# Hybrid encoder step on one core: sums of up-projection weight blocks made step by step through the mixers' phase instead of in the first up block

## The chip, the cores and the metric

The kernel runs on one core of a Trainium2 chip. The metric is device time in microseconds (us) of one execution, the median of several runs; lower is better. The core has five engines, each with its own in-order queue: PE (TensorE, matrix products), DVE (VectorE), ACT (ScalarE), POOL (GpSimd) and SP (SyncE), which here issues nearly all DMAs.

## The reference

One layer of an encoder, for a prompt of 2048 tokens and a sample group of 8 x 16 tokens, all in float32:

```python
h = rms_norm(x, norm_g[0])
z = h @ w_in                      # 1024 -> 3592, split into attention and mLSTM operands
att = band_attention(...)         # 8 heads x 64, own chunk and 8 chunks before
hb  = mlstm_sequence(...)         # 4 heads x 128, blockwise recurrence
x = x + rms_norm(concat(rms_norm(att), gated hb) @ w_out, norm_g[1])
u = rms_norm(x, norm_g[2]) @ w_up # 1024 -> 2 * 2816 (gate, up)
y = causal depthwise conv of width 3 over u, plus b_conv
x = x + rms_norm((gelu(gate of y) * (up of y)) @ w_down, norm_g[3])
```

What matters for the change is `w_up`. The kernel does its product with Strassen's method in Winograd's form: a 2 x 2 scheme of weight blocks a11, a12, a21, a22 is multiplied in 7 products instead of 8, and for this it needs four sums of weight blocks: s1 = a21 + a22, s2 = s1 - a11, s3 = a11 - a21, s4 = a12 - s2.

## The kernel before

**Phases.** The mixers' phase runs 28 groups: two halves of the tokens times 14 column groups of `w_in` (`seq`, the loop over `n_`). The matrix products of a group are the main stream. After each piece of it (`for u, (pe, dve) in enumerate(it)`, one pass per four inner products) the program calls `pump(pe, dve)` with the PE and DVE time that the piece is reckoned to cost. `pump` then takes steps from two pipelines, attention (`att_stream`) and mLSTM (`mem_stream`), as long as the reckoned DVE time stands below `SHARE` (0.615) times the reckoned PE time, two steps at most per call. Work that is put into `ahead` is made in the same pass and is counted in the same account: splitting the next group's weights, norms of the second half.

After the 28 groups comes the output projection (`project`, run through `out`): 17 tiles of 128 rows in the order 0 to 7, the sample tile (16), 8 to 15. For each tile `load` fetches the mixed row (`mr`, from `mixd`), `norm` scales it, `turn_rows` transposes it (`mT` on PE, then `mt` on ACT and DVE), 48 products make two halves (`wo`) which DVE copies out (`mx`), and the new row goes to `x2d`. The pipelines are pumped there too. When `load` comes to tile 8, `drain()` empties both pipelines at one go and `open_ffn()` closes the pools of the mixers' phase, opens those of the FFN phase, and starts `h2_units`, which fetches the rows `x2r` from `x2d` and transposes them (`h2T`) for the up product.

The FFN phase runs three blocks of tokens (b = 0, 1, 2), each with an up part (22 steps f: 7 products of 12 matmuls, then conv and GELU) and a down part.

**The weight blocks.** `load_quads(b, f, g)` fetches the 128 x 512 blocks ("quads") of step f for the first four products (g = 0) or the last three (g = 1). In block 0 it loads the four raw blocks, makes the four sums on DVE (L1274), stores each of them to `wsd[f]` in DRAM (L1276) and hands a12, a22 and s4 on through `raws`. In blocks 1 and 2 it loads all seven quads: three raw ones from `w_up` (L1269) and four sums from `wsd`. `load_up` then splits each quad into a high and a low part, on ACT (L1257) and DVE (L1258).

**Order.** The program is written in emission order. The Tile framework then places the instructions of each engine by its own reckoning of when they can run, so an instruction may stand earlier or later in its queue than it was written; `tc.keep_in_program_order` fixes a DMA's place. On the chip each engine works through its queue strictly in that order.

Of the kernel before, what the change touches and what calls it, by code (L numbers as in the profile page):

```python
# [17 lines left out]
P = 128  # L18
# [10 lines left out]
NF = 22  # L29
# [15 lines left out]
def hymba_step(ctx: ExitStack, tc: tile.TileContext, I: dict, O: dict):  # L45
# [1104 lines left out]
    def load_group(gi):  # L1150
# [19 lines left out]

        return h, l, steps()

    def norm_steps(half):

        for ci, tiles in enumerate(HALVES[half]):
            ch = phT.tile([P, 2, KT, 384], F32R, tag="hT", name=f"hT{half}_{ci}", bufs=3)
            chunks.append(ch)
            for j, t in enumerate(tiles):
                norm_tile(t, ch, j, ps_big)
                yield 0.9, 2.5  # L1180
# [9 lines left out]
        pass  # L1190
    next(norms)
    load_bias()
    for n_, (half, gi) in enumerate(seq):
        wh, wl, _ = pend
        split = iter([])
        if n_ + 1 < len(seq):
            pend = load_group(seq[n_ + 1][1])
            split = pend[2]
        g = GROUPS[gi]
        i = int(g[2])  # L1200
        nm = f"{g}_{half}"
        if g[:2] == "va":
            it = group_rows(wh, wl, half, chunks, vd[i], nm, 264 if gi == 0 else 256,
                            [O["v_prompt"][i], O["v_sample"][i].unsqueeze(1)])
        elif g[:2] == "qk":
            it = group_T(wh, wl, half, chunks, [qTd[i], kTd[i]], [-(DA ** -0.5), None], nm,
                         [None, [O["k_prompt"][i], O["k_sample"][i]]])
        elif g[:2] == "qb":
            it = group_T(wh, wl, half, chunks, [[t_[:, c, :] for t_ in qkbd[i]] for c in range(2)],
                         [None, DH ** -0.5], nm)  # L1210
        else:
            it = group_rows(wh, wl, half, chunks, vobd[i], nm)
        if half == 0 and gi == 13:
            chunks = []
            norms = norm_steps(1)
        if n_ == len(seq) - 1:
            out = project([0, 1, 2, 3, 4, 5, 6, 7, SAMPLE, 8, 9, 10, 11, 12, 13, 14, 15])
            split = w_out_steps()
            next(split)
            next(out)  # L1220
        for u, (pe, dve) in enumerate(it):
            ahead = []
            if n_ < len(seq) - 1 or u >= 6:
                ahead.append(next(split, (0.0, 0.0)))
            if n_ == len(seq) - 1 and u == 12:
                ahead.append(next(out))
            if (half == 0 and gi == 13 and u >= 6 and u % 2 == 0) or (gi == 0 and u % 2 == 0):
                ahead.append(next(norms, (0.0, 0.0)))
            pump(pe + sum(a[0] for a in ahead), dve + sum(a[1] for a in ahead))
        for _ in split:  # L1230
            pass
        if gi == 0:
            if half == 0:
                nc.sync.dma_start(bgate, I["b_gate"].broadcast_to([P, 8]))
                nc.sync.dma_start(gatt, I["g_att"])
                heads.append(build_bias)
                mems.append(lambda: prep(prep_sample()))
            mems.append(lambda half=half: prep(prep_prompt(half)))
        if g[:2] == "qk":
            attention(i, half)  # L1240
            if half == 0 and i == 3:
                heads.insert(len(heads) % 4, lambda: attention_sample(0, EARLY))
            if half == 1 and i == 0:
                heads.insert(len(heads) % 4, lambda: attention_sample(EARLY, DB))
        if g[:2] == "vo":
            mems.append(lambda i=i, half=half: mlstm(i, half))
            if half == 0:
                mems.append(lambda i=i: mlstm_sample(i))
# [8 lines left out]
        nc.scalar.copy(h, r)  # L1257
        nc.vector.tensor_tensor(l, r, h, op=ALU.subtract)  # L1258

    raws = {}  # L1260

    def load_quads(b, f, g):

        src = lambda i: I["w_up"][f][:, i * 512:(i + 1) * 512]
        if b == 0 and g == 0:
            q = []
            for i in range(4):
                q.append(quad(f"wu{f}_{i}"))
                nc.sync.dma_start(q[i], src(i))  # L1269
            a11, a12, a22, a21 = q  # L1270
            s1, s2, s3, s4 = [quad(f"ws{f}_{i}") for i in range(4)]
            for o, x, y, op in ((s1, a21, a22, ALU.add), (s2, s1, a11, ALU.subtract), (s3, a11, a21, ALU.subtract),
                                (s4, a12, s2, ALU.subtract)):
                nc.vector.tensor_tensor(o, x, y, op=op)  # L1274
            for i, o in enumerate((s2, s3, s1, s4)):
                nc.sync.dma_start(wsd[f][:, i * 512:(i + 1) * 512], o)  # L1276
            raws[f] = [a12, a22, s4]
            return [a11, s2, s3, s1]
        if b == 0:
            return raws.pop(f)  # L1280
        kept = lambda i: wsd[f][:, i * 512:(i + 1) * 512]
        out = []
        for i, s_ in enumerate([[src(0), kept(0), kept(1), kept(2)], [src(1), src(2), kept(3)]][g]):
            r = quad(f"wu{b}_{f}_{g}_{i}")
            nc.sync.dma_start(r, s_)
            out.append(r)
# [399 lines left out]
```

## Time and profile before

| what | value |
|---|---|
| three runs | 2813.98 us median, 2809.69 to 2816.1 |
| span of the profiled execution, first to last instruction | 2794.3 us |
| start, first group's norms | 0 to 56.0 |
| mixers' phase, groups 1 to 27 | 56.0 to 1044.4 |
| output projection | 1044.4 to 1317.6 |
| up part, block 0 | 1317.6 to 1645.9 |
| down part, block 0 | 1645.9 to 1840.1 |
| up part, block 1 | 1840.1 to 2158.1 |
| down part, block 1 | 2158.1 to 2356.0 |
| up part, block 2 (320 columns instead of 384) | 2356.0 to 2626.1 |
| down part, block 2 | 2626.1 to 2794.3 |

The page gives no time of its own for the profiled execution beside its span. The median of the runs lies 2813.98 - 2794.3 = 19.7 us above the span: start and end of the execution, which the instructions don't cover. The stages are cut at the first matmul of each kind. A time such as 1195.58 is counted from the span's start.

In a row of a view, `L1274 DVE TENSOR_TENSOR ws<-wu,wu 128x512 ... x44 | 30.2, 687 | 7.1 <-DMA ...` means: line 1274, on DVE, writes `ws` from `wu` and `wu`, 44 times, 30.2 us in sum, 687 ns each; before them the engine was idle 7.1 us, mostly for a DMA. PEld is the loading of weights into PE, which overlaps the products. PEclk is the clock that TensorE was granted, as a share of full speed.

### The profile page before, as it was taken

Reading aid. Unit: us, or ns where it says so; the run is one execution under the profiler, and the core shown is the slowest. Engines: PE = TensorE matmul, PEld = TensorE weight load, DVE = VectorE, ACT = ScalarE, POOL = GpSimd, SP = SyncE. Lnnn points to the kernel's source line nnn. Section 1 sums busy time; section 2 is a strip of 40 time slices with the busy share of each in tenths; the row PEclk is TensorE's granted clock in tenths of the full one; section 3 lists DMA queues with packets and bytes.
Section 4 is the critical chain, followed back from the end, with each engine's and each line's share of the span. In section 5 each row is a group of like instructions: output and inputs, shape, how many; then the busy total and the mean of one; then the engine's idle time right before and its main releaser. Section 6 shows DMA issues by size and latency. Waiting matters only on the chain.

```text
span 2794.3 us, 47075 instructions
## 1 busy us (share of the span) xinstructions
PE 2728.0 (98%) x16587; PEld 2551.0 (91%) x16587; DVE 1873.5 (67%) x3442; ACT 1408.9 (50%) x2836; POOL 449.9 (16%) x876
## 2 busy tenths in 40 slices
PE   8999999999999999999999999999999999999998
PEld 7999999998899998878999988899999778999887
DVE  5344455656456678666989986467777854888855
ACT  4445555644356676443454556345445543555543
POOL 1000010212000012344212210011111310222221
PEclk9999999999999999999999999999999999999999
DMA  5544355557554555255645455644444774555585
GB/s 189 157 123 126 111 173 157 171 159 212 165 159 147 159 183 165 91 194 210 192 164 173 162 171 173 220 148 157 151 153 154 259 262 158 169 180 177 182 309 195
DMA packets 313419, 486.04 MB, mean 174 GB/s; under 512 B 55427, under 2 KB 150623, under 8 KB 313055
## 3 DMA queue, kind: packets, MB, share of 16 engines
q1 hardware_dynamic: 274590, 449.21, 50.2%
q10 hardware_dynamic: 38592, 33.83, 3.6%
q8 instruction: 130, 2.13, 0.3%
q14 instruction: 107, 0.87, 0.1%
HBM read 359.36 MB, written 126.70 MB: 174 GB/s over the span
## 4 chain that ended last, share of the span: by engine, by line
PE 52%; DVE 4%; DMA 2%; issue 2%; ACT 1%; POOL 1%; SPq 0%; DVEq 0%; POOLq 0%; ACTq 0%
PE uec L95 6%; PE uec L96 6%; PE uec L97 5%; PE dn L97 4%; PE dn L96 3%; PE dn L95 3%; PE ua L97 3%; PE ua L95 3%; PE ua L96 3%; PE dnm L95 2%; PE dnm L97 2%; PE dnm L96 2%; PE wo L95 2%; PE wo L96 2%; PE wo L97 2%
## 5 line engine op out<-in xcount | busy, mean ns | idle before, releaser
L95 PE MATMUL uec<-B,wuh 128*128 128x384 f32 (+1 forms) x720 | 236.6, 329 | 5.6 <-DVE uu L1499 4.7
L96 PE MATMUL uec<-B,wuh 128*128 128x384 f32 (+1 forms) x720 | 235.4, 327 | 0.0
L97 PE MATMUL uec<-B,wul 128*128 128x384 f32 (+1 forms) x720 | 233.5, 327 | 0.0
L1258 DVE TENSOR_TENSOR gl<-gr,gh 128x768 fp32r<-128x768 f32 (+3 forms) x141 | 118.3, 846 | 158.6 <-ACT gh L1257 158.2
L1257 ACT CAST gh<-gr 128x768 fp32r<-128x768 f32 (+3 forms) x141 | 102.1, 736 | 211.5 <-PE dn L96 178.3
L1257 ACT CAST wuh<-wu 128x512 fp32r<-128x512 f32 x255 | 141.8, 617 | 91.2 <-PE uec L96 87.3
L95 PE MATMUL dn<-wdh,gh 128*128 128x512 f32 x466 | 182.6, 392 | 2.4 <-DVE ug L1410 2.4
L96 PE MATMUL dn<-wdl,gh 128*128 128x512 f32 x466 | 183.6, 394 | 0.0
L97 PE MATMUL dn<-wdh,gl 128*128 128x512 f32 x466 | 168.5, 396 | 0.0
L1258 DVE TENSOR_TENSOR wul<-wu,wuh 128x512 fp32r<-128x512 f32 x255 | 164.7, 685 | 2.8 <-DMA x2d<-mx 2.8
L393 DVE CUSTOM_DVE_ANT_0 tmp<-s,nb 128x640 f32<-128x640 f32 (+4 forms) x128 | 94.5, 738 | 95.8 <-PE s L383 95.2
L95 PE MATMUL vo<-wi_h,hT 128*128 128x256 f32 x544 | 156.0, 287 | 0.6 <-DVE mt L199 0.6
L97 PE MATMUL vo<-wi_h,hT 128*128 128x256 f32 x544 | 156.4, 287 | 0.0
L96 PE MATMUL vo<-wi_l,hT 128*128 128x256 f32 x544 | 155.5, 286 | 0.0
L95 PEld LDWEIGHTS uec<-B,wuh 128*128 128x128 f32 x720 | 135.3, 188 | 9.9 <-DVE uu L1499 6.7
L96 PEld LDWEIGHTS uec<-B,wuh 128*128 128x128 f32 x720 | 135.5, 188 | 0.1
L97 PEld LDWEIGHTS uec<-B,wul 128*128 128x128 f32 x720 | 135.2, 188 | 0.0
L95 PE MATMUL qk<-hT,wi_h 128*128 128x384 f32 (+1 forms) x384 | 128.5, 335 | 4.3 <-ACT qk_st L224 3.4
L406 DVE TENSOR_TENSOR ptl<-pt,pth 128x640 fp32r<-128x640 f32 (+4 forms) x128 | 93.7, 738 | 57.6 <-ACT pth L405 56.5
L394 ACT ACTIVATE tmp<-tmp,mn 128x640 f32<-128x640 f32 (+4 forms) x128 | 97.6, 763 | 63.0 <-DVE mn L393 60.5
L96 PE MATMUL qb<-hT,wi_h 128*128 128x384 f32 (+1 forms) x384 | 128.0, 333 | 0.0
L96 PE MATMUL qk<-hT,wi_h 128*128 128x384 f32 (+1 forms) x384 | 127.6, 332 | 0.0
(409 smaller groups left out, 8901.6 us busy)
## 6 DMA issues: line engine op xcount, KB each, us to landing
wu<-in_w_up SPq DMA_DIRECT2D x220, 256.0 KB, 3.9
wu<-wsd SPq DMA_DIRECT2D x176, 256.0 KB, 4.0
wdr<-in_w_down SPq DMA_DIRECT2D x132, 256.0 KB, 5.5
gr<-gd SPq DMA_DIRECT2D x78, 384.0 KB, 3.5
wi_raw<-in_w_in SPq DMA_DIRECT2D x52, 512.0 KB, 4.0
wsd<-ws SPq DMA_DIRECT2D x88, 256.0 KB, 2.8
gd<-g SPq DMA_DIRECT2D x44, 384.0 KB, 3.4
kraw<-kTd SPq DMA_DIRECT2D x112, 128.0 KB, 3.3
```

The lines of the kernel that those rows point to most:

```text
L95: nc.tensor.matmul(out, ah, bh, start=start, stop=False, skip_group_check=onto)
L96: nc.tensor.matmul(out, ah, bl, start=False, stop=False, skip_group_check=onto)
L97: nc.tensor.matmul(out, al, bh, start=False, stop=stop, skip_group_check=onto)
L393: nc.vector.tensor_tensor_reduce(o_, s_, b_, 1.0, 3e38, ALU.add, ALU.min, accum_out=mn)
L394: nc.scalar.activation(tmp[:, :n], tmp[:, :n], AF.Exp, bias=mn, scale=-1.0, accum_out=rsum[:, i % 4, hh:hh + 1])
L406: nc.vector.tensor_tensor(s.ptl[:, sl, qc], ptv, s.pth[:, sl, qc], op=ALU.subtract)
L1257: nc.scalar.copy(h, r)
L1258: nc.vector.tensor_tensor(l, r, h, op=ALU.subtract)
```

## The change

A new generator `weight_sums` makes the sums of all 22 steps during the mixers' phase. For each f it loads the four raw blocks by one DMA of 1 MB into one buffer (`wsum`, 8 KB per partition, one of it), waits five passes, makes the four sums in place on DVE, each in a pass of its own (the last shares its pass with the store), stores the whole buffer to `wsd[f]` by one DMA of 1 MB, and waits six passes: 15 passes per f, 330 in all. One step of it is taken in each pass of the groups from the second one on, and its DVE time (0.69 reckoned per sum) goes into `pump`'s account. What is left at the end of the last group is made there.

In block 0, `load_quads` no longer loads raw blocks for sums, makes sums or stores them: it loads the seven quads as the other blocks do. The order of the sums within `wsd[f]` is another, and `load_quads` follows it. Beside that the program is built with `dynamic_dma_scratch_size=1024`, which leaves more of each partition to the kernel.

```diff
+    def weight_sums():
+        for f in range(NF):
+            t = pr.tile([P, 4, 512], F32, tag="wsum", name=f"wsum{f}", bufs=1)
+            tc.keep_in_program_order(nc.sync.dma_start(t, I["w_up"][f].rearrange("p (a n) -> p a n", a=4)))
+            for _ in range(5):
+                yield 0.0, 0.0
+            a11, a12, a22, a21 = [t[:, i, :] for i in range(4)]
+            for o, x, y, op in ((a22, a21, a22, ALU.add), (a21, a11, a21, ALU.subtract), (a11, a22, a11, ALU.subtract),
+                                (a12, a12, a11, ALU.subtract)):
+                nc.vector.tensor_tensor(o, x, y, op=op)
+                if o is not a12:
+                    yield 0.0, 0.69
+            nc.sync.dma_start(wsd[f].rearrange("p (a n) -> p a n", a=4), t)
+            yield 0.0, 0.69
+            for _ in range(6):
+                yield 0.0, 0.0
...
+    sums = weight_sums()
     for n_, (half, gi) in enumerate(seq):
...
+            if n_:
+                ahead.append(next(sums, (0.0, 0.0)))
...
+        if n_ == len(seq) - 1:
+            for _ in sums:
+                pass
...
-    raws = {}
-
     def load_quads(b, f, g):
         src = lambda i: I["w_up"][f][:, i * 512:(i + 1) * 512]
-        if b == 0 and g == 0:
-            q = []
-            for i in range(4):
-                q.append(quad(f"wu{f}_{i}"))
-                nc.sync.dma_start(q[i], src(i))
-            a11, a12, a22, a21 = q
-            s1, s2, s3, s4 = [quad(f"ws{f}_{i}") for i in range(4)]
-            for o, x, y, op in ((s1, a21, a22, ALU.add), (s2, s1, a11, ALU.subtract), (s3, a11, a21, ALU.subtract),
-                                (s4, a12, s2, ALU.subtract)):
-                nc.vector.tensor_tensor(o, x, y, op=op)
-            for i, o in enumerate((s2, s3, s1, s4)):
-                nc.sync.dma_start(wsd[f][:, i * 512:(i + 1) * 512], o)
-            raws[f] = [a12, a22, s4]
-            return [a11, s2, s3, s1]
-        if b == 0:
-            return raws.pop(f)
         kept = lambda i: wsd[f][:, i * 512:(i + 1) * 512]
         out = []
-        for i, s_ in enumerate([[src(0), kept(0), kept(1), kept(2)], [src(1), src(2), kept(3)]][g]):
+        for i, s_ in enumerate([[src(0), kept(0), kept(3), kept(2)], [src(1), src(2), kept(1)]][g]):
...
-    nc = bacc.Bacc("TRN2", target_bir_lowering=False, num_devices=1)
+    nc = bacc.Bacc("TRN2", target_bir_lowering=False, num_devices=1, dynamic_dma_scratch_size=1024)
```

How the change moves instructions is seen at two places. The first is the DVE queue where the last attention unit ends and the FFN phase is opened, in the middle of the output projection. `attst3` is the last attention result; `x2r0`, `x2r3` are the first rows of the FFN phase; `mr8`, `mr9` are tiles 8 and 9 being scaled for the projection; a copy of `wo7` or `wo16` into `mx` follows 24 projection products of that tile on PE. Before:

```order
L436 TENSOR_TENSOR attst3_3_15157<-ao3_3_15152,rinv3_3_15150 128x512
L1014 COPY mx7_15107<-wo7_1_15191 128x512
L1042 MEMSET halo_15181 128x88
L1014 COPY mx16_15253<-wo16_0_15255 128x512
L1079 SCALAR_TENSOR_TENSOR x2r0_15187<-x2r0_15187,n2_0_rs_15212,g2_15183 128x1024
L1079 SCALAR_TENSOR_TENSOR x2r3_15189<-x2r3_15189,n2_3_rs_15219,g2_15183 128x1024
L1026 SCALAR_TENSOR_TENSOR mx7_15107<-mx7_15107,n1_7_rs_15240,norm_row1_13133 128x1024
L1014 COPY mx16_15253<-wo16_1_15332 128x512
L985 TENSOR_SCALAR mr8_15185<-mr8_15185,att8_rs_15250 128x512
```

And now, the same place of the DVE queue:

```order
L436 TENSOR_TENSOR attst3_3_15326<-ao3_3_15321,rinv3_3_15319 128x512
L1042 MEMSET halo_15335 128x88
L1079 SCALAR_TENSOR_TENSOR x2r0_15341<-x2r0_15341,n2_0_rs_15366,g2_15337 128x1024
L1079 SCALAR_TENSOR_TENSOR x2r3_15343<-x2r3_15343,n2_3_rs_15373,g2_15337 128x1024
L1026 SCALAR_TENSOR_TENSOR mx7_14958<-mx7_14958,n1_7_rs_15394,norm_row1_12943 128x1024
L985 TENSOR_SCALAR mr8_15339<-mr8_15339,att8_rs_15404 128x512
L1026 SCALAR_TENSOR_TENSOR mx16_15407<-mx16_15407,n1_16_rs_15516,norm_row1_12943 128x1024
L1100 TENSOR_TENSOR B0_0_15358<-b110_15427,B0_0_15358 128x4x128
L985 TENSOR_SCALAR mr9_15468<-mr9_15468,att9_rs_15526 128x512
```

The three copies out of `wo7_1`, `wo16_0` and `wo16_1` have moved ahead of the last attention units, and the scaling of tile 9 has come up behind that of tile 8. On PE the last attention transpose (`ao3`) was followed by the rest of `wo7_1` and all of `wo16` before; those three rows and the first of `wo16` were

```order
L67 MATMUL ao3_3_15152<-ident_69,attT3_3_14865 128x128 x2
L95 MATMUL wo7_1_15191<-wo6_13608,mt7_14889 128x512
L96 MATMUL wo7_1_15191<-wo6_13608,mt7_14889 128x512
L97 MATMUL wo7_1_15191<-wo6_13608,mt7_14889 128x512
L95 MATMUL wo16_0_15255<-wo0_13395,mt16_15099 128x512
```

and now it is followed at once by what hangs on the FFN phase's first rows and on tiles 8 and 9:

```order
L67 MATMUL ao3_3_15321<-ident_69,attT3_3_15177 128x128 x2
L1087 MATMUL h2T_pt0_0_0_15422<-ident_69,x2r0_15341 128x128 x4
L1087 MATMUL h2T_pt0_1_0_15443<-ident_69,x2r3_15343 128x128 x4
L1087 MATMUL h2T_pt0_1_1_15483<-ident_69,x2r3_15343 128x128 x4
L67 MATMUL mT8_pt0_15457<-ident_69,mr8_15339 128x128 x8
L67 MATMUL mT9_pt0_15571<-ident_69,mr9_15468 128x128 x8
L1087 MATMUL h2T_pt0_0_1_15556<-ident_69,x2r0_15341 128x128 x4
L95 MATMUL wo8_0_15531<-wo0_13221,mt8_15399 128x512
```

No projection product stands between the last attention transpose and `wo8` any more. The second place is the DVE queue at the end of the first group, near 43 us. `gates` are copies out of the group's accumulators, `xr16` is the sample tile on its way to its transpose `hT`. Before:

```order
L273 COPY gates_328<-va0_0_5_669 128x8
L219 SCALAR_TENSOR_TENSOR xr16_731<-xr16_731,n0_16_rs_737,norm_row0_352 128x1024
L273 COPY gates_328<-va0_0_6_718 128x8
L273 COPY gates_328<-va0_0_7_767 128x8
L199 TENSOR_TENSOR hT0_2_632<-hT16_pt0_740,hT0_2_632 128x8x128
```

And now:

```order
L273 COPY gates_328<-va0_0_5_669 128x8
L1183 TENSOR_TENSOR wsum0_845<-wsum0_845 128x512 x4
L273 COPY gates_328<-va0_0_6_718 128x8
L219 SCALAR_TENSOR_TENSOR xr16_731<-xr16_731,n0_16_rs_737,norm_row0_352 128x1024
L273 COPY gates_328<-va0_0_7_767 128x8
L199 TENSOR_TENSOR hT0_2_632<-hT16_pt0_740,hT0_2_632 128x8x128
```

The four sums of f = 0 have come to stand ahead of the sample tile's scaling, and on SP the 1 MB load of `wsum0` stands just ahead of the load of `xr16`.

## The prediction

> **What bounds the kernel now.** I read the page's head first, then the busy time by stages, then who waits for whom on PE.
>
> ```profile
> span 2794.3 us, 47075 instructions
> ...
> PE 2728.0 (98%) x16587; PEld 2551.0 (91%) x16587; DVE 1873.5 (67%) x3442; ACT 1408.9 (50%) x2836; POOL 449.9 (16%) x876
> ```
>
> PE is the bound: it stands idle for 2794.3 - 2728.0 = 66.3 us. The change takes no matrix product away, so all it can win or lose is idle time of PE and products that run slowly. The two up parts of equal work, and the mixers' phase and the projection ahead of them, by stage (length, then busy time of PE, PEld, DVE, ACT, POOL, granted clock, DMA share and GB/s):
>
> ```profile
> 56.00:1044.40 988.40, 967.94 (x6980) 943.08 (x6981) 542.57 (x1356) 516.89 (x1251) 83.01 (x256) 1.00 0.52 158
> 1044.40:1317.60 273.20, 264.81 (x1414) 222.78 (x1414) 190.62 (x299) 129.72 (x311) 99.59 (x133) 0.99 0.49 159
> 1317.60:1645.90 328.30, 321.61 (x1825) 316.74 (x1823) 301.25 (x455) 166.80 (x267) 70.42 (x87) 1.00 0.54 177
> ...
> 1840.10:2158.10 318.00, 317.99 (x1825) 317.67 (x1823) 246.00 (x367) 162.90 (x271) 42.94 (x96) 1.00 0.48 154
> ```
>
> Block 0 (third row) takes 328.30 us for the 1825 products that block 1 (fourth) does in 318.00, without any idle time. Its DVE is busy for 301.25 of 328.30 us. Who PE waits for in block 0:
>
> ```profile
> PE uec L95 <- DVE uu L1499: 4.7, 6, 1.6
> PE ua L97 <- DVE wul L1258: 1.6, 1, 1.6
> PE ub L97 <- DVE wu L1258: 0.2, 1, 0.2
> ```
>
> All three are waits for DVE, 6.5 us. So the change aims at a true cost, and that cost is small.
>
> **Block 0.** The sums leave it:
>
> ```profile
> L1274 DVE TENSOR_TENSOR ws<-wu,wu 128x512 f32<-128x512 f32 x44 | 30.2, 687 | 7.1 <-DMA wu<-in_w_up 7.1
> ```
>
> That group is half of the 88 sums; at 687 ns, 88 make 60.5 us. DVE falls from 301.25 to about 241 us, below block 1's 246.00. Per step, block 0 moves 7 quads in instead of 4 in and 4 out, as block 1 does without making PE wait. I take block 1 as its twin: 318.00 - 328.30 = **-10.3 us**. It can't be much more, since block 1 has nothing left to lose.
>
> **The projection.** The account of `pump` is where the price lies. The sums' 60 us are counted as DVE work, so attention and mLSTM get fewer steps during the 28 groups and more of them are left for the projection. There `drain()` makes the rest at one go. What that does is seen in the queue of PE: before, the last attention unit was followed by the rest of tile 7 and all of tile 16; now those products stand ahead of the last units, and nothing but dependent work stands between them and tile 8. The chain that ended last has the same place in before (start, length):
>
> ```profile
> 1195.58 0.70 DVE attst L436
> ...
> 1196.30 0.56 SPq L440
> ...
> 1196.91 0.62 SPq L1044
> ...
> 1198.07 6.72 DMA x2r<-x2d
> ...
> 1204.87 1.16 ACT sq L1075 x2
> ...
> 1209.07 1.28 DVE mx L1026
> 1210.35 0.60 DVE mx L1014
> 1210.95 2.42 DVE mr L985
> ...
> 1213.41 1.98 PE mT_pt L67 x8
> ...
> 1215.42 1.02 ACT mt L198
> ...
> 1216.48 0.80 PE wo L95
> ```
>
> SP stores `attst` and only then, in its queue, fetches the FFN's first rows `x2r`; DVE scales tile 8 (`mr`) behind them. From `attst` to the first product of tile 8 that is 1216.48 - 1195.58 = 20.9 us. In before most of it is covered. The projection's products alone, and then everything, in those stretches:
>
> ```profile
> 1195.30:1207.30 12.00, 12.00 (x52) 9.48 (x51) 1.39 (x2) 0.00 (x0) 1.00 0.56 171
> ```
>
> ```profile
> 1195.30:1216.50 21.20, 16.48 (x79) 13.28 (x77) 11.47 (x14) 9.11 (x20) 9.82 (x14) 0.90 0.50 157
> ```
>
> 52 products cover 12.00 us, and PE idles 21.20 - 16.48 = 4.7 us. Now the cover is gone, as these products are made earlier, where PE had next to no idle time for them to fill: +12.0. The chain also grows: DVE has the `mx` of tile 16 (1.28) and the scaling of tile 9 (2.42) ahead of what tile 8 waits for, and one copy of `wo16_1` (0.60) less: +3.1. The transposes of tile 9 are work done meanwhile; I take half of 1.98, -0.9. Together **+14.2**. If every one of the chain's steps kept its length but the growth fell away, it would be +11; a cover that is partly kept is excluded by the order. That the x2r load takes 6.72 us is the softest part: 2 us either way.
>
> Ahead of `attst`, the last six units run without projection products between them too. What that costs shows where before had one such place:
>
> ```profile
> PE mT_pt L67 <- DVE mr L985: 3.0, 1, 3.0
> PE pt L67 <- DVE ptl L406: 1.8, 1, 1.8
> PE h2T_pt L1087 <- DVE x2r L1079: 1.4, 1, 1.4
> ```
>
> PE stood 1.8 us for the split of the unit before (second row). Between the last six `pt` two gaps hold nothing else (2 x 1.8), and three hold a group of twelve `ot` products, which takes 1168.68 - 1167.35 = 1.3 us:
>
> ```profile
> 1167.35 0.28 PE L418 MATMUL ot<-pth,vhl 128*128 128x256 f32 x1
> ...
> 1168.68 0.52 PE L67 MATMUL pt<-ident,tmp 128*128 128x128 f32 x3
> ```
>
> That leaves 3 x 0.5; with some 1.1 for the last sum and copy before `attst` it makes 6.2, less the 1.8 that before paid: **+4.4**, between 0 (DVE keeps up) and 6 x 1.8 = 10.9.
>
> After such a pause PE is slow for a while. The granted clock behind the 3.0 us wait (third figure from the end):
>
> ```profile
> 1212.00:1216.00 4.00, 2.59 (x12) 2.42 (x12) 3.85 (x5) 1.04 (x3) 3.27 (x5) 0.54 0.47 165
> 1216.00:1219.00 3.00, 2.75 (x8) 2.05 (x7) 2.54 (x3) 3.00 (x7) 0.88 (x1) 0.50 0.72 193
> 1219.00:1222.00 3.00, 3.00 (x13) 2.37 (x13) 3.00 (x3) 1.04 (x2) 2.98 (x2) 0.97 0.95 326
> ```
>
> Before pays this already: 0.54 and 0.50 up to 1219, then 0.97. I count nothing for it twice. The Trainium skill (TensorE: Matmul & The Clock Gate, Part 1) says that PE falls to half its clock after an idle window of about 3.4 us and needs about 3.4 us of sustained work to come back; the rows above agree. By that rule the early pause below, which before has too short to trip it, would also cost half of 3.4 us, and the sum would stand 1.7 us higher.
>
> **The start.** The first 1 MB load stands just ahead of the sample tile's load on SP, which ACT waits for and on which PE's transpose hangs:
>
> ```profile
> 36.13 0.33 SPq L212 DMA_DIRECT2D xr<-in_x_sample  x1
> ```
>
> ```profile
> 41.16 1.06 ACT L216 ACTIVATE hT<-xr 128x1024 fp32r<-128x1024 f32 x1 [4.01 <-DMA xr<-in_x_sample]
> ```
>
> ```profile
> 47.98 0.39 PE L95 MATMUL va<-wi_h,hT 128*128 128x264 f32 x1 [1.10 <-ACT hT L198]
> ```
>
> PE already waits at the end of it. At 326 GB/s with a DMA share of 0.95 (the 1219 to 1222 row), the full rate is some 343 GB/s, so 1.05 MB ahead of the sample tile means 3.1 us; the four sums ahead of it on DVE fall into that time. **+3.1**, 0 if the loads overlap, 5.8 if the sums (4 x 0.687) come on top.
>
> **The rest of the mixers' phase.** The change adds 60.5 us to 542.57 of DVE in 988.4: 61% busy instead of 55. All transfers taken together, it adds 22 x 2 MB here, of which a part makes waits that PE has already:
>
> ```profile
> PE cus L781 <- DMA cs<-in_state_c: 5.8, 6, 2.0
> ```
>
> 46 MB at 343 GB/s are 134 us of all DMA engines, on a share of 0.52: 0.66. A sum that reaches DVE before its load holds up all that is queued behind it there, the splits and softmax steps that PE waits for; in block 0 that took 7.1 us for 44 sums (the L1274 row), and the five passes between load and sum are there to prevent it. Raising the 5.8 us by half gives **+3**. Bounds: -5, as the idle time of 20.5 us here is shuffled anew, to +14 (7.1 / 44 x 88).
>
> **The scratch** serves transfers described by software; the page's queues are hardware ones or instruction fetches, so it moves no time:
>
> ```profile
> q1 hardware_dynamic: 274590, 449.21, 50.2%
> q10 hardware_dynamic: 38592, 33.83, 3.6%
> q8 instruction: 130, 2.13, 0.3%
> q14 instruction: 107, 0.87, 0.1%
> ```
>
> **Sum.** -10.3 + 14.2 + 4.4 + 3.1 + 3 = +14.4 us. The span becomes 2808.7 us, and with the same 19.7 us around it the median 2813.98 + 14.4 = **2828.4 us**, 0.5% slower.
>
> **Rivals.** *Faster, through the mixers' phase.* Steps spread thinner over the groups give attention more products to hide behind; the 20.5 us of idle time between 56 and 1044.4 would shrink. It decides once it returns more than the +14.4 and 5.6 beyond, 20 us, that is nearly all of it: 2814.0 + 14.4 - 3 - 20.5 = 2804.9 us. For it speaks that the pipes get fewer steps per pass; against it, that the account holds the DVE share where it was, and that part of the idle time hangs on DMAs. *No change.* The uncovered chain is short: the x2r rows land sooner (SP's queue is emptier there), the tail before `attst` costs nothing, the start overlaps. 12.0 + 3.1 - 0.9 - 3.2 (half of the 6.72) - 10.3 = +0.7: 2814.7 us. For it: four of my terms are soft; against it, that the cover of 12 us alone outweighs block 0. *Slower by far.* DVE waits for the 1 MB loads throughout and passes it on: +14 instead of +3, and the tail at its upper end: 14.4 + 11 + 6.5 = +32, 2846 us. For it: one buffer, and loads four times as large; against it, five passes of lead. *Not what it says.* Block 0 stays at 328.30 because conv and splits alone hold PE: 2838.7 us. Against it stands block 1 with the same work.
>
> **How the numbers follow.** Forecast (+6 to +25 us): 0.66, with the last rival, whose time lies in it. No change: 0.13. Faster: 0.09. Slower by far: 0.12. The range runs from 2810, inside the no-change case, to 2845, at the edge of the far one. Three runs of before spread by 0.23%, so 0.2%, 5.6 us, is about what a measurement of this kernel can tell from no change. Slower by more than that: 0.66 + 0.12 = 0.78; within: 0.13; faster: 0.09.
>
> **What would show it.** Right: block 0 at 318 us with no waits for DVE; a pause of PE of some 20 us between the last `ao` and `wo` of tile 8, its releasers `mr`, `x2r` and `mt`; a sample tile that lands near 44 us. Wrong: `wo` products after the last attention unit, a pause under 10 us there, or idle time between 56 and 1044 that has changed by more than 10 us.

## The result, and the profile after

Four runs of the changed kernel took 2853.3 us in the median (2842.5 to 2857.97), beside 2811.84 us for the kernel before on the same chip: a ratio of 1.0147, 95% interval 1.012 to 1.0173, that is +41 us (34 to 49). Slower, as forecast, but nearly three times the +14.4 of the sum, and past the 2845 us at which the forecast's range ended. Among all runs below one execution was in a slow state, 9242 us of e_nodma, and it is left out.

The head of the page and the mean clock, answering to those of before:

```profile
span 2856.2 us, 47175 instructions
...
PE 2750.5 (96%) x16587; PEld 2566.8 (90%) x16587; DVE 1874.2 (66%) x3442; ACT 1409.0 (49%) x2836; POOL 426.1 (15%) x876
```

```profile
core 0: 2856.2 us, clock 0.987
```

```profile
core 0: 2794.3 us, clock 0.997
```

The second row is before's. PE idles 105.7 us instead of 66.3, and the same 16587 products keep it busy 22.5 us longer. The profiled execution of before was a quick one: the 19.7 us between its span and the median of the runs are not start and end of the execution, for after's profiled execution took 2857.97 us with a span of 2856.2, 1.8 us apart. This shifts no difference in the forecast. From here on the base is a second profile of the same order of instructions, taken from the kernel before with the small scratch (e_scratch, below; span 2804.7 us). The stages of the base, then of after: start, mixers' phase, output projection, up part of block 0 (length, then busy time of PE, PEld, DVE, ACT, POOL, then granted clock, DMA share, GB/s):

```profile
0.00:56.00 56.00, 42.52 (x313) 40.61 (x313) 29.98 (x47) 27.35 (x47) 9.62 (x33) 1.00 0.51 172
56.00:1051.20 995.20, 972.54 (x6980) 947.60 (x6981) 542.70 (x1356) 516.50 (x1251) 84.40 (x256) 0.99 0.52 157
1051.20:1323.20 272.00, 263.61 (x1413) 221.56 (x1412) 190.55 (x299) 129.51 (x311) 99.51 (x132) 0.99 0.49 159
1323.20:1653.40 330.20, 321.79 (x1825) 316.73 (x1824) 301.67 (x456) 167.48 (x268) 74.02 (x87) 1.00 0.54 176
```

```profile
0.00:56.00 56.00, 41.04 (x282) 39.55 (x283) 32.50 (x49) 26.65 (x44) 9.63 (x33) 0.94 0.67 223
56.00:1072.20 1016.20, 975.26 (x6943) 946.28 (x6942) 576.94 (x1423) 505.84 (x1232) 88.53 (x255) 0.99 0.63 195
1072.20:1384.70 312.50, 282.75 (x1482) 235.58 (x1481) 202.31 (x313) 140.86 (x331) 98.23 (x134) 0.95 0.44 141
1384.70:1703.40 318.70, 318.25 (x1825) 317.65 (x1823) 253.62 (x371) 168.12 (x267) 43.96 (x87) 1.00 0.53 167
```

Block 0 falls from 330.20 to 318.70 us, with 0.45 us of idle time left. Everything ahead of it takes 61.5 us more (1384.7 against 1323.2). Some 70 products have slid from the first two stages into the projection, so the stages can't be compared by length alone; the three together have 8706 products in the base and 8707 in after. For these, PE is busy 1299.05 us instead of 1278.67: **20.4 us of slower products**. The other **41.1 us are idle time**: 19.76 more in the first two stages (55.90 against 36.14), 21.36 more in the projection (29.75 against 8.39).

The clock accounts for most of the slower products, though not for all of them. The trace records the stretches at half clock; up to the up part PE is busy for 46.1 us inside them in after and for 19.8 in the base. At half clock half of that time is lost, 23.1 against 9.9 us: an estimate of 13.2 of the 20.4 us. For the other 7.2 no cause was found.

Two places show how. In the mixers' phase, what DVE waits for (us in total, times, longest) has a new row:

```profile
DVE wsum L1183 <- DMA wsum<-in_w_up: 29.8, 16, 6.6
```

In 16 of the 21 steps of this stage (the first step falls into the start) DVE reaches the first sum before its 1 MB has landed. In the projection, the stretch from the last `attst` to the first product of tile 8, in before and in after, and pieces of the latter:

```profile
1195.58:1216.48 20.90, 16.18 (x75) 12.98 (x73) 11.45 (x14) 9.09 (x20) 9.82 (x14) 0.90 0.50 155
```

```profile
1260.19:1285.34 25.15, 7.49 (x32) 6.33 (x33) 13.97 (x13) 7.37 (x14) 12.46 (x14) 0.50 0.57 176
...
1263.00:1267.00 4.00, 0.00 (x0) 0.00 (x0) 0.00 (x0) 0.00 (x0) 0.00 (x0) 0.50 1.02 269
...
1272.00:1276.00 4.00, 2.36 (x10) 1.58 (x9) 2.74 (x3) 2.18 (x4) 3.66 (x7) 0.50 0.25 103
...
1285.00:1289.00 4.00, 4.00 (x16) 3.29 (x15) 3.94 (x5) 2.41 (x4) 0.00 (x0) 0.69 0.89 251
```

The chain is 4.25 us longer, PE idles 17.66 us in it instead of 4.72, and what it does there it does at 0.50 of the clock, until the products of tile 8 follow each other again (0.69 in the last row).

### The profile page after: what moved, and what is told of

It is laid out like the page before. It is cut to its first block, busy times and chain, and to the rows that moved or that the text cites. A ratio compares the mean times of both kernels' runs of the same rounds, so it can differ in the third digit from the quotient of the medians.

```text
span 2856.2 us, 47175 instructions
## 1 busy us (share of the span) xinstructions
PE 2750.5 (96%) x16587; PEld 2566.8 (90%) x16587; DVE 1874.2 (66%) x3442; ACT 1409.0 (49%) x2836; POOL 426.1 (15%) x876
## 4 chain that ended last, share of the span: by engine, by line
PE 56%; DMA 2%; DVE 2%; ACT 1%; issue 1%; POOL 1%; SPq 0%; DVEq 0%; POOLq 0%; ACTq 0%
PE uec L95 6%; PE uec L96 6%; PE uec L97 6%; PE dn L97 3%; PE dn L96 3%; PE dn L95 3%; PE ua L97 3%; PE ua L96 3%; PE ua L95 3%; PE dnm L95 2%; PE dnm L97 2%; PE wo L95 2%; PE wo L96 2%; PE wo L97 2%; PE dnm L96 2%; PE ub L96 1%
## 5 line engine op out<-in xcount | busy, mean ns | idle before, releaser
L1281 ACT CAST wuh<-wu 128x512 fp32r<-128x512 f32 x315 | 173.0, 617 | 78.6 <-PE uec L96 74.8
L1282 DVE TENSOR_TENSOR wul<-wu,wuh 128x512 fp32r<-128x512 f32 x315 | 201.9, 684 | 2.8 <-DMA x2d<-mx 2.8
L95 PE MATMUL qk<-hT,wi_h 128*128 128x384 f32 (+1 forms) x384 | 130.5, 340 | 8.8 <-ACT qk_st L226 8.1
L1281 ACT CAST wu<-wu 128x512 fp32r<-128x512 f32 x147 | 84.8, 617 | 98.2 <-PE uec L96 64.0
L97 PE MATMUL qk<-hT,wi_l 128*128 128x384 f32 (+1 forms) x384 | 129.2, 337 | 0.0
```

The lines of the kernel that those rows point to most:

```text
L95: nc.tensor.matmul(out, ah, bh, start=start, stop=False, skip_group_check=onto)
L97: nc.tensor.matmul(out, al, bh, start=False, stop=stop, skip_group_check=onto)
```

## The experiments

Ratios are to the kernel before, in runs on the same chip, with their 95% intervals. "Theory" and "rival" are those of each expectation; they changed as the runs came in. Several of these kernels take raw blocks or zeros where the sums belong; they show time only.

### Taking parts away in the order that the scheduler makes

**e_scratch**: the kernel before with `dynamic_dma_scratch_size=1024`.

> The kernel before with the dynamic-transfer scratch at 1 KB and nothing else. Theory: no transfer uses it, so the time is that of before within 0.2%, and the profile is a second look at before. Rival: the other place of the buffers moves the time by more than 0.2%.

2804.14 us, ratio 0.9999 (0.9989 to 1.0009). The scratch moves no time.

**e_noacct**: the sums are made, but not counted.

```diff
-                    yield 0.0, 0.69
+                    yield 0.0, 0.0
...
-            yield 0.0, 0.69
+            yield 0.0, 0.0
```

> The changed kernel with the sums counted at 0 in the pump's account instead of 0.69 each; all else as changed. Theory (the account starves the pipes, and the drain in the projection pays): the stage from the first product of the output projection to the first of the up part falls from 312.5 us to 275 to 290, while the mixers' phase keeps its loss (first projection product near 1072 us); in all 2815 to 2830 us. Rival (the projection is slow for its long DMA chain or DVE order, not for the account): that stage stays above 300 us, 2845 us or more.

2836.14 us, 1.0113 (1.009 to 1.0135); first product of the projection at 1064.8 us, projection 298.8 us with 1462 products. The theory's 275 to 290 us and 2830 us were missed, but part of the loss goes with the account. But the written order of attention is now that of before, and still some 50 products slide into the projection: the account is not their only cause.

**e_nodma** and **e_nodma2**: of the 1 MB transfers, the first keeps one load and one store, the second one store alone, with the buffer set to zero once; the up products take raw blocks where the sums belong. The main lines of the second:

```diff
-            tc.keep_in_program_order(nc.sync.dma_start(t, I["w_up"][f]...))
+            if f == 0: nc.vector.memset(t, 0.0)
-            nc.sync.dma_start(wsd[f]..., t)
+            if f == NF - 1: nc.sync.dma_start(wsd[f]..., t)
```

> The changed kernel with the sums made and counted as there, but on one buffer that is loaded once and stored once: 21 of the 22 pairs of 1 MB transfers are left out, and the up parts load raw weight blocks in place of the sums, so the up products are not those of the reference. Theory A (the transfers delay other loads in the mixers' phase): first projection product at 1045 to 1055 us instead of 1072, the projection stage stays near 310 us, in all 2825 to 2835 us. Theory B (the DVE work, or the new order of the queues, makes the loss in the mixers' phase): first projection product stays at 1065 to 1075 us, 2845 us or more.

> The kernel after without the 22 pairs of 1 MB transfers (one store is left): the sums are made of a buffer of zeros, with their account, and the up products take raw blocks in place of the sums, so the output of the FFN part is another. Theory (DVE work and its account cost about half of the mixers' loss and most of the order change in the projection): first wo product at 1056-1064 us, projection 295-312 us, time 2836-2844 us. Rival (the transfers carry the mixers' loss): first wo product at 1054 us or before, time under 2832 us.

2839.91 us over three runs, 1.0129 (1.0112 to 1.0145), and 2840.11 us, 1.0132 (1.0117 to 1.0148). In the second the projection starts at 1055.7, 4.5 us behind the base, and takes 312.3 us: sums and account alone bring the projection's whole loss, and little of the mixers'. That is the order's work: from the projection on PE has the very order of after, and no 1 MB load was made.

**e_dmaonly**: the transfers without sums and account; e_noacct, with the sums left out as well.

```diff
-                nc.vector.tensor_tensor(o, x, y, op=op)
```

> The changed kernel with the 22 pairs of 1 MB transfers alone: no sums are made in the mixers' phase and none is counted, so wsd holds raw blocks and the up products are not those of the reference. Theory A (transfers): first projection product at 1060 to 1075 us, projection stage 275 to 285 us, in all 2815 to 2825 us. Theory B (DVE work): first projection product at 1040 to 1050 us, in all 2800 to 2808 us, that is before less block 0's 10 us.

2825.46 us, 1.008 (1.0063 to 1.0097); projection at 1051.9, 301.7 us long, with 1483 products. Neither theory's stages came: the projection starts 8 us earlier than the one for the transfers said and is 17 us longer. The parts add up to more than the whole: +22 us for the transfers alone and +37 for sums and account alone, each with block 0's gain, against +41. In all these kernels Tile places the instructions anew, so no part is taken away alone.

One reading avoids the products that slide between the stages: in each of them the up part starts after the same 8703 recorded products. Behind the base's 1323.2 us it starts 30.5 us later in e_dmaonly, 40.5 in e_noacct, 44.8 in e_nodma2 and 61.5 in after (57.8 in its repeat, e_after2). With the orders that the scheduler makes, then, the transfers bring about half, the sums beside them 10 and the account 21 us more.

### The cover in the projection

**e_pin16**: after, with the products of the sample tile kept behind the last `ao` on PE.

```diff
+                    with tc.issue_after(heads_end[0].ins) if t == SAMPLE else nullcontext():
                         mm3(acc, s.mt[:, 0, k, :], ...)
```

> The kernel after, whole, with one edge more on PE: the 48 products of the sample tile (wo16) stand behind the last attention transpose (ao3) in PE's queue, as 51 products did before. Theory (the uncovered chain behind the last attention unit and the half clock that follows it are the projection's cost): the pause in h2T and mT falls from 17 to under 8 us, the granted clock of the projection rises from 0.95 to 0.97 or more, the stage falls from 312.5 to 285-295 us (the 69 products that slid into it from the mixers' phase stay, some 18 us), and the time to 2826-2836 us. Rival (the order is a symptom; what costs is attention that was left over and transfers in the way): the wait only changes its place, the stage stays at 305 or more and the time at 2845 or more.

2840.7 us, 1.0129 (1.0114 to 1.0144). The same stretch, from the last `attst` to tile 8, and the whole projection:

```profile
1243.36:1261.92 18.56, 15.79 (x72) 12.40 (x70) 9.13 (x11) 8.20 (x18) 8.15 (x12) 0.91 0.54 165
```

```profile
1065.40:1365.80 300.40, 281.64 (x1482) 233.06 (x1481) 200.04 (x314) 141.12 (x332) 99.36 (x134) 0.98 0.46 147
```

The pause is gone (2.77 us idle), the clock is back at 0.91, and the stage is 12.1 us shorter with as many products. Up to the projection all five queues have the order of after. So the lost cover is a true cost, though the stage missed the 285 to 295 us expected, and the time missed 2836. **e_pindma** does the same to e_dmaonly:

> e_dmaonly (22 pairs of 1 MB transfers, no sums made and none in the account, so raw blocks stand where the sums belong and the FFN's output is another) with wo16 kept behind the last ao3. Theory (the lost cover is a cost of its own, whatever has moved the order): projection 288-295 instead of 301.8 us, time 2812-2820 us. Rival (attention that slid into the projection is all of it): projection 299 us or more, time 2823 us or more.

2823.53 us, 1.0078 (1.0063 to 1.0093). The stage falls by 7.8 to 293.9 us as expected; the time missed the 2820 expected, and the median can't be told from e_dmaonly's.

### The mixers' phase, with the order left to the scheduler

**e_after2** is after again:

> The kernel after once more, unchanged, for a second profile and for a comparison on the same chip with the kernels beside it: 2842-2857 us, first wo product at 1062-1076 us, projection 308-315 us.

2848.78 us, 1.0166 (1.015 to 1.0182), projection at 1070.0, as expected. Its queues have the order of after.

**e_pinlate** is e_pin16 with a later start:

```diff
-            if n_:
+            if n_ >= 4:
                 ahead.append(next(sums, (0.0, 0.0)))
```

**e_split** is after with each block loaded in a pass of its own, and each sum stored as it is made:

```diff
-            tc.keep_in_program_order(nc.sync.dma_start(t, I["w_up"][f]...))
+            for i in range(4):
+                tc.keep_in_program_order(nc.sync.dma_start(t[:, i, :], I["w_up"][f][:, i * 512:(i + 1) * 512]))
+                yield 0.0, 0.0
...
+                nc.sync.dma_start(wsd[f][:, i * 512:(i + 1) * 512], o)
```

> As e_pin16, and the sums start with the fifth group instead of the second (354 passes are left for 330 steps). Theory (the first 10 us of the mixers' loss come from 1 MB loads in the way of the start, with the norms and the mLSTM's first state going through DRAM at the same time): the fifth group starts within 3 us of before's, the later loss stays, and the time is 6 to 11 us under e_pin16's. Rival (each pair of transfers costs the same wherever it stands): the first wo product comes as late as in e_pin16, within 3 us, and so does the time.

> The kernel after, with each 1 MB load as four of 256 KB in four successive passes, and each store as four of 256 KB, each with its sum. The queues' order elsewhere is as in after. Theory (a 1 MB transfer stands in front of the small ones that ACT and DVE wait for, 7.4 us to landing): the wi_raw loads land in about 4.3 instead of 5.3 us, ACT's waits for them fall from 61 to under 45 us, the mixers' phase shortens by 8-15 us, and the time comes to 2838-2846 us. Rival (it is the bytes, or the DVE work, not the size of a piece): the mixers' phase within 4 us of 1016.2 and the time within 4 us of 2853.

Both fell. e_pinlate took 2865.67 us, 1.0221 (1.0205 to 1.0236). Its fifth group starts 2.3 us behind the base's (after: 11.4, its repeat: 7.7), so the early loss does come with the first sums and their loads; but more attention is left over, 1578 products in a projection of 327.9 us. e_split took 2884.52 us, 1.0283 (1.0266 to 1.03), the slowest of the scheduled ones: the `wi_raw` loads land in 4.0 us instead of 5.3, yet DVE waits for the blocks as in after (30.4 us against 29.8) and ACT's waits for `wi_raw` rise (60.9 us against 55.8). The order elsewhere was expected to be that of after; it isn't. Of 1472 DVE instructions up to the projection, 946 stand in the same sequence. So the size of a piece was not tested alone.

**e_pinsum** puts the first sum of each step behind the DVE instruction written last before it; **e_pinboth** has that and the edge of e_pin16.

```diff
+                with tc.issue_after(last_dve()) if o is a22 else nullcontext():
                     nc.vector.tensor_tensor(o, x, y, op=op)
```

> The kernel after, with the first sum of each step kept on DVE behind the DVE instruction that was written last before it, so that the order can't pull it up to the load: the five passes of lead come back. Theory (transfers alone and sums alone cost little up to the first wo product, 0.6 and 4.5 us, but both together 14 to 21, because DVE stands waiting for the 1 MB loads with other work behind it): DVE's waits for wsum fall from 32.9 to under 8 us, the mixers' phase is 8-15 us shorter than in the repeated run of after, and so is the time. Rival (these waits lie in DVE's slack, and what costs is the order of attention): the waits fall, but the time stays within 4 us of the repeated run.

> e_pin16 and e_pinsum together. Theory (two separate costs that add): 18-28 us under the repeated run of after, and at least 8 us under e_pin16's 2840.7, that is 2820-2832 us. Rival (one effect hides the other, or the order moves elsewhere): 2837 us or more.

2859.2 us, 1.0203 (1.0187 to 1.0219), and 2844.29 us, 1.0156 (1.0138 to 1.0174). DVE's waits for the loads fell from 33.6 us in e_after2 only to 20.6 in 8 waits, and the time rose: the theory missed. The two have the same order on all five queues up to the projection, and it began at 1079.5 us in one profile and at 1058.5 in the other. Nor is e_pinsum's order that of after (998 of 1472 DVE instructions in the same sequence). A difference of some 10 us in this phase can't be read from single profiles of such kernels; this pair leaves the question open. e_pinboth's 2844.29 missed its 2820 to 2832 us.

### Nearly the same order, with and without

To hold the order still, Tile's own reckoning is turned off, so that each queue stands as written:

```diff
-    with tile.TileContext(nc, schedule_with_timeline_sim=True) as tc:
+    with tile.TileContext(nc, schedule_with_timeline_sim=False) as tc:
```

Such a kernel is slower as a whole; what counts is the difference. **e_nsb** is the kernel before so built, **e_nsan** is e_noacct, **e_nsa** is after with its account.

> The kernel before with the Tile framework's own reckoning of the order turned off (schedule_with_timeline_sim=False): each engine's queue follows the order in which the program is written. It is the base for the two runs beside it; 2800-2870 us. No theory speaks of its distance to before, only of theirs to it.

> The kernel after with the same option off and the sums counted 0 in the account, so that all five queues stand as in e_nsb but for the sums, their transfers and what block 0 no longer does (69 of 9871 rows of PE differ). Theory (order: most of the 61 us that after loses up to the up part comes from instructions put in another order, not from the sums and transfers as such): the up part starts at most 15 us later than in e_nsb, block 0 is 6-12 us shorter, and the time is between 8 us below and 8 us above e_nsb's. Rival (contention: 46 MB more and 60 us of DVE more hold up the queues in any order): the up part starts 25 us later or more, the time is 15 us or more above e_nsb's.

> The kernel after with the same option off, its account kept: the sums' time in the account makes the program take attention and mLSTM steps later, so the written order itself differs from e_nsb's (2523 rows of PE). Theory (order): 8 us or more above e_nsan. Rival (contention): within 5 us of e_nsan.

2899.8 us (2898.94 to 2903.16), 2933.99 us (2929.99 to 2939.46) and 2938.12 us (2930.61 to 2943.09): +34 us in nearly the same order. It is not quite the same: up to the projection 7198 of PE's 7340 instructions in e_nsan, 1336 of DVE's 1423 and 1249 of ACT's 1315 stand in the sequence of e_nsb, and the others have moved. My theory at that point, that the order was the cost, fell as far as this goes: the time came past the rival's bound of 15 us. The account's own order adds little here (e_nsa's interval, 1.0444 to 1.0504, holds e_nsan's 1.047). So built too, **e_nsd** (e_dmaonly) has only the transfers, and **e_nsz** (e_nodma2, not counted) only the sums, made of zeros; their queues lie nearer to e_nsb's (7264 and 7302 of PE's instructions in its sequence).

> The order as written (as e_nsb and e_nsan), with the 22 pairs of 1 MB transfers alone: no sums are made, raw blocks stand in their place, so the FFN's output is another. The base is e_nsb; e_nsan, with transfers and sums, had its first wo product 37.1 us later than the base, growing by some 1.7 us with each pair and flat after the last. Theory (interaction: the sums stand on DVE waiting for their loads, 43 us in 16 waits): the first wo product at most 10 us later than in e_nsb, time at most 2905 us. Rival (the bytes: the transfers alone delay the small ones that ACT and DVE wait for): 25 us later or more, time 2918 us or more.

> The order as written, with the 88 sums alone, counted 0 and made of a buffer of zeros that stays in place: no 1 MB loads, one store, raw blocks in place of the sums in the up products, so the FFN's output is another. Theory (interaction): the first wo product at most 12 us later than in e_nsb, and together with e_nsd's delay less than two thirds of the 37.1. Rival (DVE's 60 us of work alone): 25 us later or more.

2913.7 us (2906.73 to 2917.89; ratio 1.0377, 1.0349 to 1.0405) and 2898.2 us (2892.94 to 2902.16; 1.0329, 1.0303 to 1.0355). All the time up to the projection, in e_nsb, then e_nsd, e_nsz and e_nsan:

```profile
0.00:1089.20 1089.20, 1025.95 (x7336) 995.23 (x7337) 586.19 (x1423) 557.39 (x1313) 93.36 (x293) 0.99 0.52 153
```

```profile
0.00:1109.70 1109.70, 1037.69 (x7336) 1004.21 (x7337) 587.15 (x1423) 558.75 (x1313) 92.94 (x293) 0.98 0.61 192
```

```profile
0.00:1092.10 1092.10, 1028.64 (x7336) 996.53 (x7337) 641.32 (x1512) 558.89 (x1313) 96.41 (x293) 0.99 0.52 153
```

```profile
0.00:1126.40 1126.40, 1039.15 (x7337) 1004.40 (x7338) 637.17 (x1511) 557.94 (x1313) 96.08 (x293) 0.98 0.61 189
```

The work of PE is the same in all four. 55 us of DVE work cost 2.9 us; 46 MB of transfers cost 20.5; both cost 37.2, so 13.8 come only with both, when sums must wait for their loads; what the small moves in the order add to that is not separated. These are single profiles. The medians order the four in the same way (+14, +34 and -2 us to e_nsb), on two chips between which the kernel before moved by 2.8 us. As ratios only e_nsan's 1.047 stands clear of e_nsb's 1.0349 (1.0329 to 1.0368); the intervals of e_nsd and e_nsz overlap it. By the medians the joint part is 34.2 - 13.9 + 1.6 = 22 us, less block 0's gain, which this sum takes off twice: block 0 takes 330.8 us in e_nsb and 326.8 to 327.6 in the three others, so some 18 us are left. How far the first product of some groups (counted from 0) lies behind e_nsb's, in us:

```
group            5     10     15     20     24     27   projection
e_nsd          0.4    6.2    9.8   14.4   18.7   19.5   20.4
e_nsz          2.3    1.0    0.7    1.4    1.0    1.3    2.9
e_nsan         6.6   12.4   22.0   29.8   36.1   36.0   37.1
```

The loss grows evenly while the sums are made and stops with the last (the last 1 MB load of e_nsan is issued at 938.4, group 24 starts at 964.4): 1.7 us for each of the 22 steps. What such a step looks like on SP and DVE in e_nsan (start, length):

```profile
80.94 0.59 SPq L1177 DMA_DIRECT2D wsum<-in_w_up  x1
90.78 0.69 DVE L1183 TENSOR_TENSOR wsum<-wsum 128x512 f32<-128x512 f32 x1 [7.24 <-DMA wsum<-in_w_up]
```

DVE had come to the sum 7.24 us early and stood, with the next steps of the mLSTM's gates queued behind it. Over the phase, e_nsan's row of such waits:

```profile
DVE wsum L1183 <- DMA wsum<-in_w_up: 43.2, 16, 7.2
```

The transfers alone hold up ACT, which waits for smaller loads in the same queue (`mvo` and `svr` 256 KB, `wi_raw` 512 KB); its three largest such waits up to 1130 us in e_nsb, then in e_nsd:

```profile
ACT mvo L648 <- DMA mvo<-vobd: 42.5, 23, 5.5
ACT wi_h L1167 <- DMA wi_raw<-in_w_in: 34.9, 22, 3.4
ACT svh L901 <- DMA svr<-in_cache_v: 34.2, 14, 4.9
```

```profile
ACT mvo L648 <- DMA mvo<-vobd: 49.6, 23, 5.7
ACT svh L901 <- DMA svr<-in_cache_v: 41.3, 13, 6.0
ACT wi_h L1167 <- DMA wi_raw<-in_w_in: 39.6, 23, 4.3
```

111.6 us become 130.5. The loads themselves land later: `wi_raw` in 4.9 us instead of 4.3, `svr` in 4.6 instead of 3.6, `mvo` in 3.5 instead of 3.3 (medians). In e_nsan the three waits make 116.4 us, so there DVE's own wait is the larger new one. Of e_nsd's 20.5 us, 8.8 are idle time of PE (63.25 to 72.01); the other 11.7 are the same products taking longer (1025.95 to 1037.69). PE is busy at half clock for 37.4 us instead of 16.1, which loses some 10.7 us more: the added pauses are paid a second time, most of it through the clock.

### All at once

**e_best**: the sums count 0 and start with the fifth group, the first of each step is kept back on DVE, and the sample tile is kept behind the last `ao`.

> The kernel after with all that has helped or may help at once: the sums counted 0, started with the fifth group, the first sum of each step behind the DVE instruction written before it, and wo16 behind the last ao3. If the costs found so far are separate: early loss gone (-7), cover back (-11), less attention left for the projection (-8), that is 2818-2826 us. Rival (each edit only moves the order to another place of the same kind): 2835 us or more.

2826.08 us, 1.0087 (1.0062 to 1.0111), at the upper edge of what was expected. After stands at 1.0147 and, repeated, at 1.0166, so two fifths to a half of the loss can be taken out, and it is still 23 us slower than before. No version tried beats the kernel before.

## Why the prediction was right and wrong

**Block 0, -10.3: right.** 330.20 to 318.70 against the base, 328.30 to 318.70 against before's page: -9.6 to -11.5. What PE still waits for there is a single row:

```profile
PE ua L97 <- DVE wul L1282: 0.4, 1, 0.4
```

**The start, +3.1: the wait right, the clock behind it left out.** The sample tile's square began at 41.16 in before, and in after 3.5 us later, near the 44 us forecast:

```profile
44.69 1.06 ACT L216 ACTIVATE hT<-xr 128x1024 fp32r<-128x1024 f32 x1 [4.98 <-DMA xr<-in_x_sample]
```

But PE's pause for it (3.03 us) is followed by 6.83 us at half clock, where the base has full clock up to 56 us:

```profile
48.13 1.68 PE L67 MATMUL hT_pt<-ident,xr 128*128 128x128 f32 x8 [3.03 <-DVE xr L219]
```

```profile
48.48:55.31 6.83, 5.73 (x21) 5.33 (x20) 1.22 (x1) 1.01 (x1) 0.00 (x0) 0.50 0.64 196
```

Behind it the same product stands 4.95 us later than in the base (the 291st at 57.42 against 52.48 us). The forecast named this cost, 1.7 us on top of the 3.1, and left it out of its sum.

**The projection, +14.2 and +4.4: the mechanism right, the pause nearly so.** The forecast pause stands where it was put, with the releasers named (us in total, times, longest):

```profile
PE h2T_pt L1087 <- DVE x2r L1079: 12.4, 2, 11.2
PE mT_pt L67 <- DVE mr L985: 8.1, 4, 4.6
```

The chain grew by 4.25 us (forecast +3.1), PE's idle time in it by 12.9 (forecast +14.2), and the stage's by 21.4 (forecast 14.2 + 4.4 = 18.6); e_pin16 took the pause away. One reason given was too narrow: that the price lies in the account of `pump`. With it the up part starts 21 us later than without (after against e_noacct), but without the account (e_noacct) or without sums (e_dmaonly) products of attention slide into the projection too, and part of the cover is lost; it is the placing of instructions that reacts to any addition.

**"I count nothing for it twice": wrong.** The forecast took the slow clock after a pause as already paid in before. It measured 0.50 for the 25 us of the pause and 0.95 over the stage, against 0.99, and 0.987 over the execution against before's 0.997. Over the three stages ahead of the up part the same products took 20.4 us longer. By the recorded stretches at half clock some 13.2 us of that are the clock, spread over all three stages: 2.9 in the start, 4.0 in the mixers' phase, 6.3 in the projection. The other 7.2 stay open. The rule that I cited and set aside (the Trainium skill, TensorE: Matmul & The Clock Gate, Part 1: half clock after an idle window of about 3.4 us, full clock after about 3.4 us of sustained work) agrees with this place once it is read to its end: PE was busy 7.49 of 25.15 us, never in a sustained stretch, and stayed at 0.50. I applied it to the early pause of the start only, where half clock did come, after 3.03 us without a product, and left even that out of the sum.

**"The rest of the mixers' phase", +3: wrong, and the largest error.** The text named a test for this: idle time in the mixers' phase that has changed by more than 10 us; it went from 22.66 to 40.94. The idle time of the first two stages grew by 19.76 us; with some 3 for the start taken off, 16 to 17 are left against +3, past the +14 of the upper bound, and a part of the slower products comes on top. The step raised one wait of PE (5.8 us) by half, as if the transfers touched one load. e_nsd shows that they slow several kinds of smaller loads, at some 20 us, and e_nsan that DVE stands in wait for its own loads, 14 to 18 us more. The five passes of lead, on which I relied against the far rival, last some 14 us on average in after (21 steps of 15 passes between the issues at 34.99 and 909.63), but there DVE came to the first sum only 0.6 to 10.6 us after its load was issued, 6.0 in the median: less than half of the lead that was written.

The far rival had this mechanism, at 2846 us and a chance of 0.12; it came nearest to the measured 2853.3. e_nsz shows that DVE's work, whose share (55 to 61%) is the number I weighed, is nearly free (2.9 us). These sizes are from the written order. The scheduled order has the same signs: DVE's waits of 29.8 us, and ACT's three waits for `mvo`, `wi_raw` and `svr` grown from 86.2 us in the base to 126.3. That it pays the same in the same parts is inferred, not shown: e_pinsum did not reproduce it, and after's loss does not grow evenly. Its groups lie 13.4 us behind the base's at group 3, 13.6 at 17, 3.2 at 19 and 29.0 at 22.

**The scratch, 0: right** (e_scratch).

The sum up to the up part was 14.2 + 4.4 + 3.1 + 3 = 24.7 us; this pair of profiles has 61.5. The missing 36.8 are 20.4 of slower products and 16.4 of idle time, 13.7 of it in the first two stages.

## What to carry to other kernels

Work that is moved into "spare" time of a nearly full kernel can be paid through its transfers and through whoever must wait for them in order: price the loads against the smaller loads that share their queue, and ask how early a consumer really comes, not how many steps of lead were written. Where PE is at 98%, a new pause can cost twice, as here: once as idle time (41.1 us) and once as products at half clock behind it (some 13 us). When a scheduler places instructions, no part can be taken away alone; hold the order still (here, nearly, by turning its reckoning off in both kernels), check how still it is, and compare times at equal amounts of work before attributing a difference.

## What the runs showed of the hardware

PE stayed at half clock through 25 us in which it was busy for 30% of the time (7.49 of 25.15 us): short bursts of products did not bring the clock back. A pause of 3.03 us was followed by 6.83 us at half clock. The same order of instructions reached the projection at 1058.5 us in one execution and at 1079.5 in another (e_pinboth, e_pinsum); before's two profiles differ by 6.8 us there, and three profiles of after's order (after, e_after2, e_pin16) by 6.8 as well. Smaller transfers did not help here: 88 loads of 256 KB took 5.6 us each to land, against 7.4 for 22 of 1 MB, and the median was over 30 us higher, though in another order of the queues.
